# Attention scores of two heads as four products on the two 64-row halves of the matmul array

## The chip, the cores and the metric

The kernel runs on one core of a Trainium2 chip. A core has engines that run side by side, each with its own queue in fixed order: TensorE (PE, matmuls; its weight loads are shown apart as PEld), VectorE (DVE), ScalarE (ACT), GpSimd (POOL), and SyncE (SP), whose queue here issues all DMA transfers. Engines wait for each other by semaphores. The metric is the device time of one execution in microseconds (us); lower is better.

## The reference

A trunk of two layers over 1024 tokens of width 1024, with 16 heads of 64. Each layer adds a gated mixer to the residual stream.

```python
def reference(x, ...):
    for i in range(2):
        h = rms_norm(x, norm_g[i])
        o, gate = fox_mixer(h, ...) if i == 0 else dsw_mixer(h, cos, sin, ...)
        x = x + (o * silu(gate)) @ w_out[i]

def fox_mixer(h, w_in, b_f, q_g, k_g):        # layer 1: causal attention with forgetting
    q, k, v, gate, f = split(h @ w_in)        # q, k normed per head
    c = cumsum(log_sigmoid(f + b_f))          # per token and head
    s = q @ k.T * 64 ** -0.5 + c[q] - c[k]    # masked to keys <= query
    return softmax(s) @ v, gate

def dsw_mixer(h, cos, sin, w_in, q_g, k_g):   # layer 2: three groups of dilated windows
    for window, r in ((128, 1), (512, 4), (2048, 16)):
        # q, k normed and partly rotated; tokens r apart form a sequence of its own;
        # each query sees its own block of 128 keys and the block before, at most window // r back
        o_g, lse_g = banded_attention(q[g], k[g], v[g])
    return sum(softmax over g of lse_g * o_g), gate
```

All arithmetic is float32 in the reference. The kernel gets near that with split numbers: a value is written as a high and a low part, and products of parts are added.

## The kernel before

**Projections.** The input rows stand turned in SBUF as `xh` and `xl` (high and low part, tokens along the free axis). A projection of one tile of 128 tokens (`project`, L313) is 24 matmuls of 384 columns: eight blocks of the width, in each `xh` by the high and the low part of the weights and `xl` by the high part. After each six matmuls `flow.tick()` counts one slot, and what was filed for that slot with `flow.at` is written into PE's queue there: PE's order is the order of the program. So one projection tile is four slots. The other engines' orders are set by a scheduler at build time.

**The fox layer** goes over eight pairs of heads (`hp`), in each over eight tiles of 128 tokens (`t`). A projection tile gives q, k and v of two heads, k first. **The dilated layer** does the same for 24 pairs of heads and groups (`ci`); group 0 looks one block back, group 1 in every second tile, group 2 not at all.

**Heads.** For two tiles together, `heads_pair` norms and rotates q and k in `u` and writes `hl`, 16-bit: for each tile the high and low parts of k and q of both heads, `[hi(64), lo(64)]` for each head (L420 on ACT, L421 on POOL), and behind them, copied by DVE (L422), the parts of q swapped, `[lo, hi]`. One transposing DMA (L424) turns the twelve blocks into `qk_t`. In the fox layer POOL then copies the blocks of k into `kf` (L426), which holds the keys of one pair of heads side by side; the pool has two such buffers.

**Scores.** With 128 rows, `[hi, lo]` of q against `[hi, lo]` of k gives hi·hi + lo·lo, and the swapped q gives lo·hi + hi·lo: two matmuls for each head. In the fox layer `score(e, c)` does this for head `e` and a piece `c` of up to 512 keys (L619), adds the causal mask to the last block by a third matmul of an identity with `tri_b` (L622), and DVE adds the forgetting sums and takes the minimum (L624). It stands in slots of its own, one for each head and piece. In the dilated layer `score(i)` does tile `i` of the two for both heads, block by block (L798, DVE L801, ACT L802), tile 0 in one slot and tile 1 in the next.

**Behind the scores.** `p_transpose` takes exponentials (ACT, L467), writes them as high and low parts into `ph` (cast on ACT L470, difference on POOL L473; in the dilated layer L808 and L809) and turns `ph` into `ptt` by a transposing DMA (L474, L810). Some slots later `values` multiplies `ptt` by v: three matmuls of 64 or 65 columns for each block (`pv`, L481 to L483). For the fox tiles 0 to 3 both heads share one `ph` and one transposing DMA, from tile 4 on each head has its own. Tags `ph`, `p`, `ptt` and `kf` have 2, 4, 3 and 2 buffers in the first layer; the scores' PSUM pool `ps_s` has 3. The tag `kf` also serves the row of gains `gbc` of the second norm, which is loaded when the last fox projection has been issued and is read until the output projections end (L350).

Of the kernel before, what the change touches and what calls it, by code (L numbers as in the profile page):

```python
# [22 lines left out]
P = 128  # L23
# [59 lines left out]
def trunk(ctx, tc, ins, out, cfg):  # L83
# [52 lines left out]
    ident_b = const.tile([P, P], BF16, name="ident_b")  # L136
    nc.vector.tensor_copy(ident_b, ident)
    tri_b = const.tile([P, P], BF16, name="tri_b")
    nc.vector.tensor_copy(tri_b, tri)
# [45 lines left out]
    def rotary_tables():  # L185
# [5 lines left out]
        rt = lay([P, 5, 24, half], F32, name="rt", tag="kf")  # L191
# [161 lines left out]
    def load_gbc(layer):  # L353
        gbc = lay([P, D], F32, name="gbc", tag="kf")
# [41 lines left out]
    def heads_pair(gi, t, hd, kf):  # L396
# [24 lines left out]
        nc.gpsimd.tensor_sub(hl[:, :, :4, 1], u, hl[:, :, :4, 0])  # L421
        nc.vector.tensor_copy(hl[:, :, 4:], hl[:, :, 2:4, ::-1])  # L422
        qk_t = lay([P, 12, P], F16, name="qk_t", tag="qk_t")
        nc.sync.dma_start_transpose(qk_t, hl.rearrange("p i a b d -> p (i a b d)"))  # L424
        if kf is not None:
            nc.gpsimd.tensor_copy(  # L426
                kf[:, :, t * P : (t + 2) * P].rearrange("p e (i s) -> p i e s", i=2),
                qk_t.rearrange("p (i a) s -> p i a s", i=2)[:, :, :2],
            )
        return qk_t[:, :6], qk_t[:, 6:]  # L430
# [101 lines left out]
    def x_ready(t):  # L532
        if t + 2 < NT:
            load_xt(t + 2)
            split_xt(t + 2)
        if t + 1 < NT:
            row_factor(t + 1)
        if t == 1:
            load_gbc(0)
        if t == 3:  # L540
            gain_tables()
# [17 lines left out]
    def forget_sums():  # L559
        one = sb.tile([NH, 512], F32, name="one", tag="n2k", bufs=cfg["nb"])  # L560
        nc.vector.memset(one, 1.0)
        c = lay([NH, S], F32, name="fc", tag="kf")
# [32 lines left out]
    def fox_tile(hp, t, gs, qt, kf, vt, e0):  # L595
# [9 lines left out]
        def score(e, c):  # L605
            a, b = pieces[c]
            if c == 0:
                accs[e] = BIG
                st["acc"] = sm.tile([P, 2], F32, name="acc", tag="acc", bufs=8)
            if t < 2:  # L610
                if e == 0:
                    st["p"] = lay([P, 2, nk], F32, name="p", tag="p")
                p = st["p"][:, e]
            else:
                p = lay([P, b - a], F32, name="p", tag="p")
# [382 lines left out]
```

## Time and profile before

| | |
|---|---|
| median of 3 runs | 1849.05 us (1845.42 to 1851.41) |
| the profiled execution | 1848.65 us, its span 1846.9 us |
| PE busy | 1773.2 us, 13784 matmuls |
| DVE, ACT, POOL busy | 1101.9, 997.4, 976.0 us |
| DMA | 289.27 MB, 631429 packets, 510000 of them under 512 B |
| granted TensorE clock | 0.998 |

Spans on PE are pipelined: a matmul's length holds its way through the array, and the next starts long before it ends. So costs on PE are read from the distance between starts. Idle time of an engine counts only where PE waits in the end. In a row of the groups, behind the bar stand the busy time, the mean length in ns and the idle time before; `128*128` is the size of the stationary operand, the size behind it that of the moving one.

### The profile page before, as it was taken

The page shows a single profiled execution, that of the slowest core. Times are in us where ns is not written, and L with a number is a line of the kernel's source. Part 1 is how long each engine was busy: PE and PEld are TensorE (multiplying, and loading weights), DVE is VectorE, ACT ScalarE, POOL GpSimd, SP SyncE. Part 2 cuts the span into 40 slices and gives each one's busy share as a digit, 9 for nine tenths or more (in the row PEclk, how much of TensorE's full clock was granted, in tenths as well). Part 3 has the DMA queues.
Part 4 walks back from the last instruction along what each step waited for, and adds up shares of the span by engine and source line. Part 5 has one row for each costly group of instructions (what it writes and reads, how often), then busy time and mean ns, then how long its engine had stood idle before and what let it go on. Part 6 is the DMA issues. An engine that isn't in the chain of part 4 may idle for free.

```text
span 1846.9 us, 39170 instructions
## 1 busy us (share of the span) xinstructions
PE 1773.2 (96%) x13784; PEld 1648.0 (89%) x13784; DVE 1101.9 (60%) x3762; ACT 997.4 (54%) x2648; POOL 976.0 (53%) x1195
## 2 busy tenths in 40 slices
PE   6999999999988999999999999999999999999999
PEld 5997777877877889999999999999999999999899
DVE  7546655666657263356656666666676665766641
ACT  6535665666655254445655565555555555555520
POOL 4215665665654121255656655666576765766620
PEclk9999999999999999999999999999999999999999
DMA  8445988979999463346676686676776776667762
GB/s 268 124 125 127 187 176 171 190 172 181 191 174 226 135 224 126 102 110 151 130 141 132 142 183 146 141 156 148 141 147 153 165 151 139 151 148 166 167 167 92
DMA packets 631429, 289.27 MB, mean 157 GB/s; under 512 B 510000, under 2 KB 594992, under 8 KB 631232
## 3 DMA queue, kind: packets, MB, share of 16 engines
q1 hardware_dynamic: 631232, 286.77, 68.8%
q8 instruction: 108, 1.77, 0.4%
q14 instruction: 89, 0.73, 0.1%
HBM read 124.87 MB, written 37.03 MB: 88 GB/s over the span
## 4 chain that ended last, share of the span: by engine, by line
PE 52%; DMA 9%; DVE 4%; issue 3%; ACT 2%; POOL 2%; SPq 1%; POOLq 0%; DVEq 0%; ACTq 0%
PE pj L313 46%; PE s L798 3%; DMA raw<-in_w_dsw 2%; DMA ptt<-ph 2%; DMA qk_t<-hl 2%; DMA x_d<-xo 2%; POOL w L291 1%; PE ob L481 1%; PE ob L483 1%; PE ob L482 1%; PE pt L322 1%; DVE w L291 1%; DVE hl L422 0%; POOL hl L421 0%; DMA raw<-in_w_do 0%
## 5 line engine op out<-in xcount | busy, mean ns | idle before, releaser
L313 PE MATMUL pj<-w,xh 128*128 128x384 f32 (+2 forms) x5632 | 1472.2, 344 | 26.3 <-ACT w L289 11.7
L313 PEld LDWEIGHTS pj<-w,xh 128*128 128x128 f32 x5632 | 987.5, 191 | 49.4 <-ACT w L289 12.8
L313 PE MATMUL pj<-w,xl 128*128 128x384 f32 (+2 forms) x2816 | 940.3, 334 | 0.4 <-DVE xl L326 0.2
L313 PEld LDWEIGHTS pj<-w,xl 128*128 128x128 f32 x2816 | 535.5, 190 | 1.9 <-DVE xl L326 1.9
L291 POOL TENSOR_TENSOR w<-raw,w 128x384 fp32r<-128x384 f32 (+2 forms) x264 | 268.8, 1042 | 310.1 <-ACT w L289 303.2
L473 POOL TENSOR_TENSOR ph<-p,ph 128x512 f16<-128x512 f32 (+3 forms) x176 | 172.5, 994 | 127.3 <-ACT ph L470 105.0
L421 POOL TENSOR_TENSOR hl<-u,hl 128x512 f16<-128x512 f32 x128 | 150.2, 1173 | 143.9 <-ACT hl L420 143.8
L289 ACT CAST w<-raw 128x384 fp32r<-128x384 f32 (+2 forms) x352 | 160.8, 503 | 114.8 <-PE pj L313 39.9
L809 POOL TENSOR_TENSOR ph<-p,ph 128x768 f16<-128x768 f32 (+2 forms) x96 | 155.4, 1619 | 40.5 <-ACT ph L808 37.0
L481 PEld LDWEIGHTS <-ptt 128*128 128x128 f16 x1136 | 102.6, 98 | 67.7 <-DMA ptt<-ph 36.8
L802 ACT ACTIVATE p<-p,og 128x128 f32<-128x128 f32 (+1 forms) x256 | 100.9, 441 | 114.4 <-DVE og L801 112.6
L376 ACT ACTIVATE sq<-pj 128x256 f32<-128x256 f32 x256 | 96.9, 379 | 76.2 <-DVE u L371 75.0
L258 DVE TENSOR_REDUCE vm<-raw 128x1 f32<-128x256 f32 x128 | 53.6, 419 | 141.3 <-DMA raw<-in_w_dsw 112.8
L470 ACT CAST ph<-p 128x512 f16<-128x512 f32 (+3 forms) x176 | 88.7, 537 | 90.6 <-DMA ptt<-ph 89.6
L467 ACT ACTIVATE p<-p,acc 128x512 f32<-128x512 f32 (+2 forms) x192 | 110.9, 610 | 35.9 <-DVE acc L624 35.8
L420 ACT CAST hl<-u 128x512 f16<-128x512 f32 x128 | 79.5, 621 | 90.7 <-DVE u L418 73.7
L371 DVE TENSOR_TENSOR u<-pj,gr 128x256 f32<-128x256 f32 x256 | 106.8, 417 | 34.5 <-PE pj L313 33.9
L406 POOL TENSOR_TENSOR ra<-u,cs 128x128 f32<-128x128 f32 x96 | 44.5, 463 | 147.2 <-DVE u L371 145.2
L382 DVE SCALAR_TENSOR_TENSOR vt<-pj,vs,vt 128x128 f16<-128x128 f32 x192 | 67.2, 350 | 76.0 <-ACT vt L381 73.8
L482 PEld LDWEIGHTS <-ptt 128*128 128x128 f16 x1136 | 105.9, 97 | 1.7 <-issue 1.7
L483 PEld LDWEIGHTS <-ptt 128*128 128x128 f16 x1136 | 106.1, 97 | 0.0
L389 DVE TENSOR_REDUCE pj<-sq 128x8 f32<-128x512 f32 x128 | 88.3, 690 | 26.2 <-ACT sq L376 25.1
(170 smaller groups left out, 2424.4 us busy)
## 6 DMA issues: line engine op xcount, KB each, us to landing
raw<-in_w_dsw SPq DMA_DIRECT2D x96, 384.0 KB, 3.9
raw<-in_w_fox SPq DMA_DIRECT2D x32, 384.0 KB, 3.6
og_d<-og SPq DMA_DIRECT2D x64, 132.0 KB, 2.8
cmb<-og_d SPq DMA_DIRECT2D x64, 132.0 KB, 3.3
bc<-c_d SPq DMA_DIRECT2D x32, 256.0 KB, 5.2
gs_d<-ge SPq DMA_DIRECT2D x32, 192.0 KB, 2.5
xt<-in_xt SPq DMA_DIRECT2D x16, 256.0 KB, 4.0
xrow<-in_x SPq DMA_DIRECT2D x16, 256.0 KB, 4.0
```

The source lines that it names most:

```text
L289: nc.scalar.copy(w[:, 0, :n], raw[:, k % 2, :n])
L291: eng.tensor_sub(w[:, 1, :n], raw[:, k % 2, :n], w[:, 0, :n].bitcast(F32))
L313: nc.tensor.matmul(ps[:, :n], a[:, k, cols], w.slabs[k][:, j, :n], start=(k == 0 and i == 0), stop=(k == KT - 1 and i == 2))
L371: nc.vector.tensor_mul(u[:, t % 2].rearrange("p (a b) d -> p a b d", a=2), ps[:, : 4 * HD].rearrange("p (a b d) -> p a b d", a=2, b=2), gr ...
L421: nc.gpsimd.tensor_sub(hl[:, :, :4, 1], u, hl[:, :, :4, 0])
L467: nc.scalar.activation(p, p, AF.Exp, bias=acc, scale=-1.0)
L473: (nc.gpsimd if pool_l else nc.vector).tensor_sub(ph[:, e, 1, cols], p, ph[:, e, 0, cols])
L481: nc.tensor.matmul(o[:, e, :], hi, vt[:, j, e, HD:], start=(b == 0), stop=False, skip_group_check=True)
L482: nc.tensor.matmul(o[:, e, :HD], hi, vt[:, j, e, :HD], start=False, stop=False, skip_group_check=True)
L483: nc.tensor.matmul(o[:, e, :], lo, vt[:, j, e, HD:], start=False, stop=(b == n - 1), skip_group_check=True)
L802: nc.scalar.activation(p[:, e], p[:, e], AF.Exp, bias=acc[:, e : e + 1], scale=-1.0)
L809: nc.gpsimd.tensor_sub(ph[:, 1], st["p"], ph[:, 0])
```

## The change

`hl` now holds, for each tile, the high parts of k of both heads (128 wide), the low parts of both, and the same of q: four blocks instead of six. The swapped parts and L422 go. The transposing DMA turns eight blocks for two tiles instead of twelve, and puts head 0 on partitions 0 to 63 and head 1 on 64 to 127. `kf` and its copy (L426) go: keys are read from the `qk_t` of their two tiles, of which seven are kept in the first layer instead of three.

`scores` writes four products for each run of one or two key blocks (hi·hi, hi·lo, lo·hi, lo·lo), each as two matmuls of 64 rows in turn, one for each head, into two PSUM banks. So a run of keys takes eight matmuls, where two heads took four of 128 rows for any number of keys up to 512. The mask comes as two products of 64 rows for each head (`half_i`, `half_m`), which `mask_halves` makes on POOL and DVE in the first gate projection.

One call of `score` now does both heads. In the fox layer it takes a piece in one visit, the second piece two slots later (`pc=2`), and the values of both heads stand in one slot, `LS + LP + 4`, or `+ 3` for tiles 0 to 3, counted from `e0` (before `LS + LP + 2` and `+ 4` for the heads of tiles 4 to 7, and `+ 2` and `+ 3` for tiles 0 to 3). In the dilated layer both tiles of a pair are scored in one visit, at the slot where tile 1 stood. `ptt` has four buffers in the first layer instead of three. `gbc` and the rotary scratch `rt` move from the tag `kf` to `ph`, and `cmb` gets a tag of its own.

```diff
-        hl = sb.tile([P, 2, 6, 2, HD], F16, name="hl", tag="hl", bufs=cfg["hb"])
+        hl = sb.tile([P, 2, 2, 2, P], F16, name="hl", tag="hl", bufs=cfg["hb"])
         nc.vector.tensor_mul(u, u, y.unsqueeze(3).broadcast_to([P, 2, 4, HD]))
-        nc.scalar.copy(hl[:, :, :4, 0], u)
-        nc.gpsimd.tensor_sub(hl[:, :, :4, 1], u, hl[:, :, :4, 0])
-        nc.vector.tensor_copy(hl[:, :, 4:], hl[:, :, 2:4, ::-1])
-        qk_t = lay([P, 12, P], F16, name="qk_t", tag="qk_t")
+        uv = u.rearrange("p i (a e) d -> p i a (e d)", a=2)
+        nc.scalar.copy(hl[:, :, :, 0], uv)
+        nc.gpsimd.tensor_sub(hl[:, :, :, 1], uv, hl[:, :, :, 0])
+        qk_t = lay([P, 8, P], F16, name="qk_t", tag="qk_t")
         nc.sync.dma_start_transpose(qk_t, hl.rearrange("p i a b d -> p (i a b d)"))
-        if kf is not None:
-            nc.gpsimd.tensor_copy(
-                kf[:, :, t * P : (t + 2) * P].rearrange("p e (i s) -> p i e s", i=2),
-                qk_t.rearrange("p (i a) s -> p i a s", i=2)[:, :, :2],
-            )
...
+    def scores(ss, qk, i, keys, last):
+        prods = ((2, 0), (2, 1), (3, 0), (3, 1))
+        at = 0
+        for kk, j, cnt in keys:
+            for n, (qb, kb) in enumerate(prods):
+                for e in range(2):
+                    r = slice(HD * e, HD * e + HD)
+                    nc.tensor.matmul(
+                        ss[e][:, at * P : (at + cnt) * P].rearrange("p (c s) -> p c s", c=cnt),
+                        qk[r, i, qb],
+                        kk[r, j : j + cnt, kb],
+                        start=(n == 0),
+                        stop=(last and n == len(prods) - 1),
+                        skip_group_check=True,
+                    )
+            at += cnt
...
     def load_gbc(layer):
-        gbc = lay([P, D], F32, name="gbc", tag="kf")
+        gbc = lay([P, D], F32, name="gbc", tag="ph")
...
-            for i, blk in enumerate((2 + e, 4 + e)):
-                nc.tensor.matmul(s[:, : b - a], qt[:, blk], kf[:, e, a:b], ...)
+            ss = [ps_s.tile([P, 512], F32, name="s", tag="s") for e in range(2)]
+            runs = key_runs(range(a // P, b // P))
+            scores(ss, kts[t // 2], t % 2, [(kts[j // 2], j % 2, n) for j, n in runs], not last)
...
-        sl = e0 + LS
+        for c in range(len(pieces)):
+            urgent(lambda c=c: score(c), "ps", e0 + LS + cfg["pc"] * c)
         for e in range(2):
-            for c in range(len(pieces)):
-                urgent(lambda e=e, c=c: score(e, c), "ps", sl)
-                sl += 1
-            if not both:
-                urgent(lambda e=e: values(e), "pv", sl + LP)
-        if both:
-            for e in range(2):
-                urgent(lambda e=e: values(e), "pv", sl + LP + e)
+            urgent(lambda e=e: values(e), "pv", e0 + LS + LP + cfg["pe"][both][e])
...
-        for i in range(2):
-            urgent(lambda i=i: score(i), "ps", flow.now + LSD + i)
-        urgent(values, "pv", flow.now + LSD + LPD + 1)
+        urgent(score, "ps", flow.now + LSD)
+        urgent(values, "pv", flow.now + LSD + LPD)
...
-    lsd=((15, 12), (13, 11), (11, 9))    l1=dict(ga=7, kf=2, ptt=3, ph=2, p=4, qk_t=3)
+    lsd=((16, 12), (14, 11), (12, 9))    l1=dict(ga=7, ptt=4, ph=2, p=4, qk_t=7)    pc=2, pe=((4, 4), (3, 3))
```

**PE in the dilated layer, group 0 of one pair of heads.** Names with numbers are buffers; `s2` is a PSUM bank of scores, `pj` that of a projection. Before, the end of the scores of tile 0 of a pair of tiles and the start of those of tile 1:

```order
L798 LDWEIGHTS qk_t_14634
L798 MATMUL s2_14910<-qk_t_14634 128x128
L313 MATMUL pj_14868<-w_14725,xh_114 128x384 x2
L313 MATMUL pj_14868<-w_14725,xl_115 128x384
L313 MATMUL pj_14868<-w_14728,xh_114 128x384 x2
L313 MATMUL pj_14868<-w_14728,xl_115 128x384
L798 LDWEIGHTS qk_t_14634
L798 MATMUL s2_14929<-qk_t_14634 128x128
```

Now, the same border between tile 0 and tile 1 (`scores` is L461, the projection L328):

```order
L461 LDWEIGHTS qk_t_13220
L461 MATMUL s2_13487<-qk_t_13220 128x128
L461 LDWEIGHTS qk_t_13220
L461 MATMUL s2_13488<-qk_t_13220 128x128
L461 LDWEIGHTS qk_t_13220
L461 MATMUL s2_13487<-qk_t_13220 128x256
L461 LDWEIGHTS qk_t_13220
L461 MATMUL s2_13488<-qk_t_13220 128x256
```

The two heads alternate matmul by matmul between two banks, and no projection stands between the two tiles. Over the whole program PE leaves the projections 584 times before and 386 times now (stretches of other matmuls, counted in PE's queue); 192 of the 386 hold scores.

**POOL in the fox layer, first pair of heads,** tiles 4 and 5 (`hl` is L421, then L437; `ph` L473, then L512). Before:

```order
L473 TENSOR_TENSOR ph_1895<-p_1871,ph_1895 128x512
L473 TENSOR_TENSOR ph_1895<-p_1889,ph_1895 128x128
L473 TENSOR_TENSOR ph_1960<-p_1922,ph_1960 128x512
L473 TENSOR_TENSOR ph_1960<-p_1954,ph_1960 128x128
L426 COPY kf_1340<-qk_t_1796 128x2x2x128
L473 TENSOR_TENSOR ph_2019<-p_1976,ph_2019 128x512
```

Now:

```order
L512 TENSOR_TENSOR ph_1983<-p_1940,ph_1983 128x512
L512 TENSOR_TENSOR ph_1983<-p_1979,ph_1983 128x128
L512 TENSOR_TENSOR ph_1992<-p_1943,ph_1992 128x512
L512 TENSOR_TENSOR ph_1992<-p_1981,ph_1992 128x128
L512 TENSOR_TENSOR ph_2122<-p_2063,ph_2122 128x512
L512 TENSOR_TENSOR ph_2122<-p_2118,ph_2122 128x256
```

The copy of keys, which waits for a transposing DMA, is gone from between the differences.

**SP, the second pair of heads,** tiles 5 and 6. Before:

```order
L474 DMA_TRANSPOSE ptt_2924<-ph_2923 128x12x128
L474 DMA_TRANSPOSE ptt_2988<-ph_2987 128x12x128
L424 DMA_TRANSPOSE qk_t_2905<-hl_2900 128x12x128
L474 DMA_TRANSPOSE ptt_3028<-ph_3027 128x14x128
L664 DMA y_d_83<-y_3109 128x128
```

Now:

```order
L513 DMA_TRANSPOSE ptt_3146<-ph_3145 128x12x128
L439 DMA_TRANSPOSE qk_t_3110<-hl_3106 128x8x128
L513 DMA_TRANSPOSE ptt_3155<-ph_3154 128x12x128
L708 DMA y_d_83<-y_3339 128x128
L634 DMA bc_3512<-c_d_85 128x512
```

The transfer of q and k has eight blocks instead of twelve, and stands ahead of the second head's `ptt` instead of behind it.

More of the change, by code (lines that the diff above doesn't have):

```diff
@@ L539, in x_ready @@
             load_gbc(0)
+        if t == 2:
+            mask_halves()
         if t == 3:
@@ L626, in score @@
             pl = (cfg["pl"] & 1, cfg["pl"] >> 1 & 1)
-            if c < len(pieces) - 1 or both and e == 0:
-                return
             if both:
@@ L721, in trunk @@
                 with tc.high_priority(cfg["ph_"]):
-                    qts = heads_pair(0, t - 1, hd, kf)
-                for i, qt in enumerate(qts):
-                    fox_tile(hp, t - 1 + i, gsl[:, i], qt, kf, vt, flow.now - 4 + 4 * i)
+                    kts.append(heads_pair(0, t - 1, hd))
+                for i in range(2):
+                    fox_tile(hp, t - 1 + i, gsl[:, i], kts, vt, flow.now - 4 + 4 * i)
             if hp == NHP - 1:
```

123 lines of the change are left out of this document (71 added, 52 removed).

## The prediction

> **What bounds the kernel now.** I read the span on the page first, then the stages, the groups, the waits of the fox stage, and last the timeline of PE around single scores.
>
> ```profile
> span 1846.9 us, 39170 instructions
> ```
>
> ```profile
> core 0: us, PE busy (x) PEld busy (x) DVE busy (x) ACT busy (x) POOL busy (x), PEclk, DMA share, GB/s
> 0.00:40.00 40.00, 24.67 (x96) 20.57 (x96) 30.75 (x75) 23.88 (x63) 21.17 (x28) 1.00 0.82 262
> ...
> 138.00:545.00 407.00, 375.52 (x3383) 317.19 (x3383) 251.65 (x917) 250.60 (x619) 245.24 (x257) 0.99 0.87 175
> 700.00:1070.00 370.00, 368.98 (x2860) 356.12 (x2859) 207.35 (x661) 204.94 (x529) 187.33 (x226) 1.00 0.59 128
> 1070.00:1770.00 700.00, 693.17 (x5293) 658.02 (x5293) 458.37 (x1700) 388.42 (x1125) 448.95 (x609) 1.00 0.71 155
> ```
>
> PE bounds it. In the dilated layer (700 to 1770) PE idles 8 of 1070 us, so there only less work on PE, or fewer breaks in it, can bring anything. In the fox layer (138 to 545) PE idles 31.5 of 407 us, and the DMA engines are 0.87 busy, the highest share of any long stage. What PE waits for there:
>
> ```profile
> PE o L481 <- DMA ptt<-ph: 28.3, 23, 3.1
> PE s L619 <- POOL kf L426: 2.2, 2, 1.5
> ...
> ACT ph L470 <- DMA ptt<-ph: 84.3, 46, 4.0
> ...
> POOL kf L426 <- DMA qk_t<-hl: 29.0, 22, 4.2
> ...
> DVE p L624 <- POOL ph L473: 21.5, 22, 2.5
> ```
>
> 28.3 us go on `ptt`, the turned weights for the values. Their chain is DVE, ACT, POOL, SP, transposing DMA, and it is itself held up: ACT's cast waits 84.3 us until a `ph` buffer has been turned, and POOL stands 29.0 us in front of the copy into `kf`, with the differences that feed `ptt` queued behind it.
>
> **The price of a break.** Four, then eight matmuls of 128 columns amid projections:
>
> ```profile
> 1207.35 0.34 PE L313 MATMUL pj<-w,xl 128*128 128x384 f32 x1
> 1207.53 0.40 PE L798 MATMUL s<-qk_t 128*128 128x128 f16 x4
> 1207.74 0.61 PE L313 MATMUL pj<-w,xh 128*128 128x384 f32 x2
> 1208.19 0.34 PE L313 MATMUL pj<-w,xl 128*128 128x384 f32 x1
> ...
> 1208.72 0.34 PE L313 MATMUL pj<-w,xl 128*128 128x384 f32 x1
> 1208.90 0.62 PE L798 MATMUL s<-qk_t 128*128 128x128 f16 x8
> 1209.33 0.61 PE L313 MATMUL pj<-w,xh 128*128 128x384 f32 x2
> 1209.78 0.34 PE L313 MATMUL pj<-w,xl 128*128 128x384 f32 x1
> ```
>
> The columns are start, length, engine and group. From 1208.19 to 1208.72 three projection matmuls take 0.53. One score matmul is 0.22 long (221 ns below), so eight in 0.62 start 0.40/7 = 57 ns apart. The stretch with eight takes 1.06 from `xl` to `xl`; less 0.53 and 8 x 0.057 there remain 0.07. With four it is 0.84 - 0.53 - 0.23 = 0.08. So each visit away from the projections costs about 0.07 beyond its own matmuls.
>
> **The terms.** The groups that the change touches (behind the bar: busy time, mean ns, idle time before):
>
> ```profile
> L798 PE MATMUL s<-qk_t 128*128 128x128 f16 x1120 | 95.9, 221 | 5.1 <-DMA qk_t<-hl 5.1
> L619 PE MATMUL s<-kf,qk_t 128*128 128x512 f16 (+3 forms) x384 | 95.5, 330 | 3.1 <-POOL kf L426 2.2 <-DMA qk_t<-hl 0.8
> L422 DVE COPY hl<-hl 128x512 f16<-128x512 f16 x128 | 50.1, 391 | 57.3 <-POOL hl L421 55.9
> L426 POOL COPY kf<-qk_t 128x512 f16<-128x512 f16 x32 | 19.6, 611 | 32.9 <-DMA qk_t<-hl 32.8
> ```
>
> *Fewer breaks.* PE leaves the projections 386 times instead of 584: 198 x 0.07 = **-14**.
>
> *The scores themselves.* In units of 128 columns, before: fox 8 pairs x 36 blocks x 2 heads x 2 products = 1152, masks 128, dilated 1120, in all 2400 x 57 ns = 137 us. Now 2304 + 256 + 2240 = 4800 units on half the rows. If the two heads' halves run at once, that is 2400 units of time again, 137 us; if not, 137 us more. No row of before shows halves, so these are the ends: 0 and +137. What speaks for 0 beyond the arithmetic is only that consecutive matmuls use other rows and other PSUM banks. A bound for the issue comes from the values, which also load weights for every matmul:
>
> ```profile
> 1203.72 0.20 PE L481 MATMUL ob<-vt,ptt 128*128 128x65 f16 x1
> ...
> 1204.25 0.20 PE L483 MATMUL ob<-vt,ptt 128*128 128x65 f16 x1
> ```
>
> These are the first and the last of 18: 0.53/17 = 31 ns for a load and a matmul. Two of them take 62 against the 57 of a pair of 128 columns: 5 ns on 864 pairs (128 of fox blocks, 128 of masks, 608 dilated), none on the 768 pairs of 256 columns: **+4**. The Trainium skill's TensorE: Matmul & The Clock Gate (What overlaps and what doesn't) says that a weight load runs beside matmuls in flight only when their row groups differ; by it each half would stand still for its next load. The rows just quoted speak against it, since those loads and matmuls all use the same 128 rows and still pass every 31 ns.
>
> *The wait for `ptt` in the fox layer.* POOL loses the copy and the standing before it, 19.6 + 29.0 us of 407. The transposing DMAs of a pair of heads turn 144 blocks of `ph` (4 x 36) and 48 of q and k, now 32: 176 instead of 192, 8% less on the fullest resource. DVE loses L422 (391 ns for each two tiles) from the chain of `qk_t`. Against it: both heads now start together, so the second head's exponentials queue behind the first's on ACT, and tiles 4 to 7 take all four `p` buffers in the order head 0, head 1, head 0, head 1, so that DVE's next minimum waits for the second head's difference (the 21.5 us above grow, and DVE's queue with it). The values stand two slots later for head 0, in the same slot for head 1. The ends are -28 (all gone) and +14 (half as much again); I take half of it, **-14**, because two of the three links that wait (POOL, DMA) get shorter. L619's waits, 2.2 and 0.8, go with `kf`: **-2**.
>
> *The wait for `qk_t` in the dilated layer*, 5.1 us in L798's row: the first score of a pair moves one slot later and its chain loses L422 and a third of its blocks: **-4**, between -5 and 0. POOL, DVE and SP are not waited for by PE in that stage otherwise, so the later start of tile 0's exponentials (one slot, some 1.2 us) costs nothing as long as `ptt` stays ahead, as it is now.
>
> *The end of the fox layer.* `gbc` now takes one of the two `ph` buffers when the last projection is out, and keeps it. The transposes of tiles 4 to 7 of the last pair of heads come after that, eight of them, on one buffer. In that stretch (545 to 605):
>
> ```profile
> L474 SPq DMA_TRANSPOSE ptt<-ph x11: 1234/1882/4210, 545.5 to 594.1; - x11
> ...
> DMA to landing us min/median/max: 2.8/4.1/6.3
> L470 ACT CAST ph<-p x20: 294/605/619, 545.4 to 591.1; 128x512 f16<-128x512 f32 x12, 128x384 f16<-128x384 f32 x4, 128x128 f16<-128x128 f32 x2, 128x256 f16<-128x256 f32 x2
> L473 POOL TENSOR_TENSOR ph<-p,ph x21: 430/1162/1289, 544.4 to 592.6; 128x512 f16<-128x512 f32 x13, 128x384 f16<-128x384 f32 x4, 128x128 f16<-128x128 f32 x2, 128x256 f16<-128x256 f32 x2
> ```
>
> On one buffer each must pass cast (0.6), differences (1.2 to 2.3) and landing (2.8 to 4.1) before the next cast: 4.6 to 7.0, eight times 37 to 56 us. Now the 11 of the row take from 545.5 to 594.1 and 4.1 to land, 52.7; eight elevenths of that are 38. So 0 to 18 us are added, and PE reaches these values in order, with the turned rows of the output projection behind them. SP's loads of `xr` and `yt` queue behind the late transposes too. I take **+8**.
>
> *Free:* `mask_halves`, eight small operations on POOL in the first gate projection, where POOL is about half idle (21.17 of the first 40 us); without that cover some 5 us, at 0.6 each as for L426. `ptt`'s fourth buffer and seven `qk_t` only loosen. Three PSUM score buffers against two for each visit: the next visit is two slots away, two minima (0.6 each) earlier; nothing, unless DVE stands.
>
> Sum: -14 + 4 - 14 - 2 - 4 + 8 = -22. Against the span 1846.9 that is 1825; the profiled execution has 1.75 outside its span, so **1827 us**. The median of the runs, 1849.05, is 0.4 above this execution. Less than 0.3% (5.5 us) can't be told from no change.
>
> **Rivals.**
>
> *PE must run empty at each change of form* (the other side). Scores use half the rows, all else uses 128, so 192 visits change the form twice. A 128-column score is 221 ns long and the next starts after 57, so 164 are still under way: up to 384 x 0.164 = 63 us, 1827 + 63 = **1890**. It turns the gain from 57 ns a change on. The Trainium skill's TensorEngine Tiling (Array Packing), Key Properties, states such a drain. Before has one visit in another form, `128*16`:
>
> ```profile
> 88.44 0.34 PE L313 MATMUL pj<-w,xl 128*128 128x384 f32 x1
> 88.62 1.03 PE L566 MATMUL pz<-ident,zt 128*16 128x128 f32 x8
> 89.41 0.60 PE L313 MATMUL pj<-w,xh 128*128 128x384 f32 x2
> 89.85 0.34 PE L313 MATMUL pj<-w,xl 128*128 128x384 f32 x1
> ```
>
> From `xl` to `xl` 1.41; less 0.53 it leaves 0.88 for eight, 0.11 each, which is what their starts are apart (1.03 less a matmul of about 0.27, over 7). No room for 0.3 of emptying; but this narrows columns, not rows, and it is one visit. Chance 0.12, of it 0.04 for a part that ends within 0.3% of before.
>
> *The halves don't run at once*: 1827 + 137 - 4 = **1960**. For it: nothing of before shows that they do. Chance 0.07.
>
> *Each half stands for its load*: at most 31 ns (the values' distance) on 1632 pairs, 50 us, 1827 + 50 - 4 = **1873**. Chance 0.04, for the reason above.
>
> *The fox chain is not relieved*: starting both heads together eats what POOL and the DMA save, and the end of the layer costs more: 1827 + 14 + 12 = **1853**, no change. For it: ACT is on the chain with 84.3 us of waiting for `ph`, of which there are still two. Chance 0.19, a third of it slower than 1855.
>
> *The fox chain comes free*, as the DMA share falls and POOL never stands: 1827 - 14 - 8 = **1805**. Chance 0.16.
>
> **How the numbers follow.** The forecast, 1815 to 1843, has 0.42; with the freed chain 0.58 are faster by over 0.3%, and 0.02 of the unrelieved chain's near side: 0.60. Within 0.3%: 0.11 of the unrelieved chain and 0.04 of the drain, 0.15. Slower: 0.08 drain, 0.07 no overlap, 0.04 loads, 0.06 chain, 0.25. The range from 1800 to 1862 leaves out 0.03 below and about 0.17 above.
>
> **What would show it.** Two score matmuls of the two heads starting close together and a pair of 256 columns every 110 to 120 ns show the overlap; 0.07 of remainder per visit shows that no drain is paid, 0.2 to 0.4 that it is. PE's wait for `ptt` in the fox layer should be near 14, POOL's wait for `qk_t` gone, the DMA share a little lower. Eight transposes some 5 to 7 us apart at the fox layer's end, with ACT's cast waiting for each, show the single buffer. The prediction is wrong if scores take much over 140 us of PE's starts, or if PE's fox waits stay at 28.

## The result, and the profile after

The change makes the kernel slower: 1900.18 us median of 4 runs (1896.96 to 1906.78) against 1847.24 us (1842.65 to 1851.41) for the kernel before. The ratio is 1.0292, 95% interval 1.0254 to 1.0330. The prediction, 1827 us and faster, has the wrong sign, and the result lies outside its range of 1800 to 1862.

Two windows of the profile after, the prediction's fox stage and the stretch behind it, and then the second one in the profile before:

```profile
core 0: us, PE busy (x) PEld busy (x) DVE busy (x) ACT busy (x) POOL busy (x), PEclk, DMA share, GB/s
138.00:545.00 407.00, 385.44 (x4135) 341.05 (x4136) 235.16 (x863) 243.25 (x604) 221.43 (x223) 0.98 0.79 160
545.00:700.00 155.00, 130.05 (x1139) 119.75 (x1138) 67.92 (x203) 60.86 (x141) 42.67 (x44) 0.94 0.65 167
```

```profile
545.00:700.00 155.00, 140.49 (x1056) 127.12 (x1055) 85.36 (x233) 72.46 (x171) 45.61 (x49) 1.00 0.71 193
```

In the fox window PE is busier than before (385.44 against 375.52) although it gets less far. DVE, ACT and POOL are all less busy there, and the DMA share fell from 0.87 to 0.79, so none of them has become the limit by its load; whether PE waits for one of them is told by the waits. The scores' group, and then PE's waits over the whole program (us in total, times, longest):

```profile
L461 PE MATMUL s<-qk_t 64*128 64x128 f16 (+1 forms) x3008 | 163.7, 245 | 21.6 <-DVE acc L667 21.5
```

```profile
PE s L461 <- DVE acc L667: 21.5, 12, 3.3
PE o L520 <- DMA ptt<-ph: 14.8, 12, 5.9
...
PE ob L520 <- DMA ptt<-ph: 5.5, 5, 2.7
```

The wait of the fox layer's values for `ptt` was halved (14.8, 28.3 before), but PE now waits 21.5 us for DVE to empty a score bank, for which the profile before has no row. The three rows make 41.8 us, where before the rows for `ptt`, `qk_t` and `kf` made 36.4 (28.3 + 5.1 + 0.8 + 2.2). So waits alone can't explain 53 us. Where the time is lost is seen better from the lengths of the stages. The table counts PE's projection matmuls and takes the time from the first of a stage to the first of the next, so that the same work is compared; the last row is what is left between the first projection matmul of the program and the last. It is read from one trace each, and has two of the experiments beside the two kernels:

| us | before | after | whole products | gains in a buffer of their own |
|---|---|---|---|---|
| fox layer | 435.1 | 449.1 | 423.7 | 453.5 |
| end of the fox layer (its output projection) | 132.8 | 150.0 | 149.6 | 139.1 |
| dilated layer | 961.9 | 978.2 | 948.9 | 977.1 |
| all the rest | 304.7 | 306.9 | 309.2 | 306.2 |

So 14 us were lost in the fox layer, 17 at its end and 16 in the dilated layer (the two traces are 48 us apart, the medians 53).

A part of the first two is the clock. At the end of the fox layer the column PEclk fell from 1.00 to 0.94. The trace's clock record has it as stretches of 3.4 or 6.8 us at half clock; before has two of them (6.8 us, both in the fox layer), the kernel after nine (five in the fox layer and four at its end, 17 us each, none in the dilated layer). Each of the nine begins 2 to 4 us after PE began a wait of about 2 us or more, but not every such wait is followed by one. In such a stretch a projection follows the other in 0.32 us instead of 0.175:

```profile
634.09 0.52 PE L328 MATMUL pj<-w,xl 128*128 128x384 f32 x1
634.41 0.84 PE L328 MATMUL pj<-w,xh 128*128 128x384 f32 x2
635.05 0.52 PE L328 MATMUL pj<-w,xl 128*128 128x384 f32 x1
```

So up to 45% of a stretch is lost. As an estimate that is at most 5 us more than before in the fox layer (17 against 6.8 us of such stretches) and 7 at its end, where PE idles for 2 of the 17 anyway.

In the dilated layer PE's waits for other engines are nearly as before (8.3 us from 700 to 1740, 6.6 before), so there it is likely that the visits themselves have become dearer. This is PE's timeline around one visit of the dilated layer in the kernel after, 24 products in 12 pairs:

```profile
1015.72 0.34 PE L328 MATMUL pj<-w,xl 128*128 128x384 f32 x1
1015.99 1.06 PE L461 MATMUL s<-qk_t 64*128 64x128 f16 x24
1016.97 0.62 PE L328 MATMUL pj<-w,xh 128*128 128x384 f32 x2
1017.44 0.34 PE L328 MATMUL pj<-w,xl 128*128 128x384 f32 x1
```

From `xl` to the scores it takes 0.27 us, where projections follow each other every 0.17 to 0.18. Singly, the records show the two heads' matmuls starting 3 to 4 ns apart and the pairs every 56 ns (128 columns) or 109 ns (256 columns). So the overlap of the two halves is full, and no weight load stands in its way (two loads of 94 ns belong to each pair). From `xl` to `xl` it is 1.72 us; less 0.53 for the three projections and 8 x 0.056 + 4 x 0.109 = 0.88 for the pairs, 0.31 remain, where the kernel before had 0.07. The prediction had written that 0.2 to 0.4 here would show the emptying of PE.

### The profile page after: what moved, and what is told of

Its sections match the earlier page's. It is cut to its first block, busy times and chain, and to the rows that moved or that the text cites. A ratio compares the mean times of both kernels' runs of the same rounds, so it can differ in the third digit from the quotient of the medians.

```text
span 1895.2 us, 42233 instructions
## 1 busy us (share of the span) xinstructions
PE 1817.3 (96%) x15416; PEld 1694.9 (89%) x15416; DVE 1044.1 (55%) x3637; ACT 984.4 (52%) x2648; POOL 957.4 (51%) x1171
## 4 chain that ended last, share of the span: by engine, by line
PE 55%; DMA 17%; POOL 8%; issue 7%; ACT 6%; DVE 5%; SPq 2%; POOLq 0%; ACTq 0%; DVEq 0%
PE pj L328 48%; DMA ptt<-ph 8%; DMA raw<-in_w_fox 3%; PE s L461 3%; POOL ph L512 3%; POOL w L306 3%; DMA raw<-in_w_dsw 2%; ACT ph L509 2%; ACT p L506 2%; POOL hl L437 1%; DMA x_d<-xo 1%; DVE p L667 1%; PE ob L520 1%; PE ob L522 1%; PE ob L521 1%
## 5 line engine op out<-in xcount | busy, mean ns | idle before, releaser
L328 PE MATMUL pj<-w,xh 128*128 128x384 f32 (+2 forms) x5632 | 1458.3, 342 | 23.3 <-ACT w L304 10.5
L328 PEld LDWEIGHTS pj<-w,xh 128*128 128x128 f32 x5632 | 997.4, 191 | 60.5 <-issue 14.0
L328 PE MATMUL pj<-w,xl 128*128 128x384 f32 (+2 forms) x2816 | 941.6, 334 | 0.1
L328 PEld LDWEIGHTS pj<-w,xl 128*128 128x128 f32 x2816 | 537.5, 191 | 0.4 <-DVE xl L341 0.4
L512 POOL TENSOR_TENSOR ph<-p,ph 128x512 f16<-128x512 f32 (+3 forms) x176 | 170.7, 991 | 189.6 <-ACT ph L509 167.6
L437 POOL TENSOR_TENSOR hl<-u,hl 128x512 f16<-128x512 f32 x128 | 150.6, 1177 | 99.3 <-ACT hl L436 97.9
L461 PE MATMUL s<-qk_t 64*128 64x128 f16 (+1 forms) x3008 | 163.7, 245 | 21.6 <-DVE acc L667 21.5
L461 PEld LDWEIGHTS <-qk_t 64*128 64x128 f16 x3008 | 108.1, 94 | 71.8 <-issue 61.1
L520 PEld LDWEIGHTS <-ptt 128*128 128x128 f16 x1136 | 104.5, 99 | 49.0 <-DMA ptt<-ph 25.8
L506 ACT ACTIVATE p<-p,acc 128x512 f32<-128x512 f32 (+2 forms) x192 | 105.5, 606 | 39.6 <-DVE acc L667 38.9
L839 ACT ACTIVATE p<-p,og 128x128 f32<-128x128 f32 (+1 forms) x256 | 102.3, 441 | 36.8 <-DVE og L838 36.4
L521 PEld LDWEIGHTS <-ptt 128*128 128x128 f16 x1136 | 107.0, 98 | 1.3 <-issue 1.3
```

What stands on the lines that cost most here:

```text
L328: nc.tensor.matmul(ps[:, :n], a[:, k, cols], w.slabs[k][:, j, :n], start=(k == 0 and i == 0), stop=(k == KT - 1 and i == 2))
L437: nc.gpsimd.tensor_sub(hl[:, :, :, 1], uv, hl[:, :, :, 0])
L461: nc.tensor.matmul(ss[e][:, at * P : (at + cnt) * P].rearrange("p (c s) -> p c s", c=cnt), qk[r, i, qb], kk[r, j : j + cnt, kb], start=(n ...
L506: nc.scalar.activation(p, p, AF.Exp, bias=acc, scale=-1.0)
L512: (nc.gpsimd if pool_l else nc.vector).tensor_sub(ph[:, e, 1, cols], p, ph[:, e, 0, cols])
L520: nc.tensor.matmul(o[:, e, :], hi, vt[:, j, e, HD:], start=(b == 0), stop=False, skip_group_check=True)
```

## Experiments

**1. Whole products.** Theory 1: PE runs empty when the form changes. Theory 2: the loss lies in the buffers and in DVE. In this kernel the order, the visits, the buffers and the passes of columns of the change stay; each pair of 64-row products becomes one product of 128 rows. It leaves out half of the score products and mixes the heads, so its time is no time for the task.

```diff
-                for e in range(2):
-                    r = slice(HD * e, HD * e + HD)
-                    nc.tensor.matmul(ss[e][...], qk[r, i, qb], kk[r, j : j + cnt, kb], start=(n == 0), ...)
+                e = n % 2
+                nc.tensor.matmul(ss[e][...], qk[:, i, qb], kk[:, j : j + cnt, kb], start=(n < 2), ...)
```

> The changed kernel, in which every pair of 64-row score products (one per head, on the two halves of the array) is one product of all 128 rows; so is each pair of mask products. The number of passes of columns, the visits, the buffers, the transfers and the work of DVE, ACT and POOL stay. It leaves out half of the score products and mixes the heads in the others, so its time is no time for the task. Theory 1 (PE runs empty when the rows of a product change from 128 to 64 and back): the remainder per score visit falls from 0.30 us back to 0.07, which over 192 visits is 45 us, so about 1855 us. Theory 2 (the loss comes from DVE's late minimum, the third PSUM buffer and the end of the fox layer, the form costs nothing): only the issue of 864 products goes, under 5 us, so 1895 to 1900.

Measured: 1843.3 us, ratio to before 0.9970 (0.9954 to 0.9986), 57 us less than the changed kernel and 12 below theory 1's 1855. A visit with the same passes as the one above, and then this kernel's largest waits of PE:

```profile
1003.80 0.34 PE L328 MATMUL pj<-w,xl 128*128 128x384 f32 x1
1003.97 1.06 PE L460 MATMUL s<-qk_t 128*128 128x128 f16 x12
1004.79 0.60 PE L328 MATMUL pj<-w,xh 128*128 128x384 f32 x2
1005.23 0.34 PE L328 MATMUL pj<-w,xl 128*128 128x384 f32 x1
```

```profile
PE s L460 <- DVE acc L664: 25.6, 18, 3.4
PE o L519 <- DMA ptt<-ph: 17.5, 8, 5.8
```

The twelve whole products take the same 1.06 as the twelve pairs, but the stretch from `xl` to `xl` is 1.43 instead of 1.72. The missing 0.29 is 0.10 on the way in (0.17 against 0.27), 0.16 on the way out (0.82 from the first score to the next projection, against 0.98) and 0.03 at the second projection. Of the 0.31 that remained, 0.02 are left, not the 0.07 that theory 1 took. Times 192 visits that is 56 us, and 57 were measured. The fox layer's waits for DVE and for `ptt` didn't shrink (they grew by 4 and 3 us; the dilated values' wait for `ptt` fell from 5.5 to 1.2), so it isn't they that moved. The dilated layer is the cleaner test: no stretch at half clock in either trace, and 96 visits of 0.29, so 28 us, against 29.3 in the table. In the fox layer the 25.4 us are a balance: 28 for the visits, up to 8 for the 17 us at half clock, of which this kernel has none there, and the other way 9 for its longer waits (30.5 against 21.4 in the window of the prediction). So the agreement of 56 with 57 is in part luck. Theory 1 holds; theory 2 is out as the main cause.

**2. Two visits again.** If each visit pays, more visits must pay more. Here the products of tile 0 get a visit of their own.

```diff
+        urgent(lambda: products(0), "ps", flow.now + LSD - 1)
         urgent(score, "ps", flow.now + LSD)
```

> The changed kernel, in which the score products of a dilated piece are issued in two visits again, as in the kernel before: the same products, 96 visits more, so 192 changes of form more. Theory 1 (each visit with a change of form costs 0.30 us beside its products, 0.235 of it the change): 96 x 0.30 = 29 us longer, about 1929. Theory 2 (a visit costs the 0.07 of any visit): 7 us longer, about 1907. If the score banks' wait for DVE is relieved by taking the two tiles apart, some 5 us less in both.

Measured: 1923.32 us, ratio 1.0408 (1.0382 to 1.0435), 23 us above the changed kernel: 96 more visits at 0.24 each. The dilated layer alone grew by 21.8 (978.2 to 1000.0). This is on theory 1's side (29, or 24 with the relief of the banks; 7 without the price), and PE's wait for the score banks gave back 3.9, near the 5 expected:

```profile
PE s L461 <- DVE acc L667: 17.6, 10, 3.6
```

**3. The gains in a buffer of their own.** The end of the fox layer lost its 17 us in the run with whole products too (149.6), so it has another cause. To make room, `qk_t` has six buffers here instead of seven and `ra` and `rb` one each.

```diff
-        gbc = lay([P, D], F32, name="gbc", tag="ph")
+        gbc = lay([P, D], F32, name="gbc", tag="gbc")
-    l1=dict(ga=7, ptt=4, ph=2, p=4, qk_t=7)    ra, rb: bufs=2
+    l1=dict(ga=7, ptt=4, ph=2, p=4, qk_t=6, gbc=1)    ra, rb: bufs=1
```

> The changed kernel with a buffer of its own for gbc (it shared the two buffers of ph); to make room, qk_t has 6 buffers instead of 7 and ra and rb one instead of two. Theory A (the 17 us that the last part of the fox layer and its output projection lost come from the eight transposes that then have one ph buffer): 10 to 17 us faster, 1883 to 1890. Theory B (they come from the form of the products and from DVE's late minima there): no more than 4 us faster. Against both: one ra buffer may hold POOL up, which would cost a few us.

Measured: 1886.21 us, ratio 1.0205 (1.0181 to 1.0229), 14 us less than the changed kernel; the end of the layer takes 139.1 instead of 150.0 (by these traces the fox layer ahead of it is 4 us longer). The transposing DMAs and ACT's casts there, first in the changed kernel and then here:

```profile
L513 SPq DMA_TRANSPOSE ptt<-ph x9: 1315/1567/1754, 569.9 to 628.2; - x9
...
  ACT ph L509: 14.0, 7
  PEld L520: 6.7, 2
  PE o L520: 6.2, 2
```

```profile
L513 SPq DMA_TRANSPOSE ptt<-ph x10: 1273/1802/4787, 562.0 to 614.4; - x10
```

The indented rows say who waited for these DMAs. With one `ph` buffer the transposes are 58.3/8 = 7.3 us apart, ACT's next cast waits for seven of them, 14.0 us in all, and PE's values for two, 6.2 us. With two they are 52.4/9 = 5.8 apart, and ACT and PE have no such rows; PE's 8.7 us of waits for DVE at the score banks there are gone too. Theory A holds. The size, 11 by the stage and 14 by the medians, lies in the upper part of the 0 to 18 that the prediction gave, of which it took 8. Of the 17 us some 6 stay (139.1 against 132.8). This run has 16 us at half clock there, like the changed kernel, and before none; that is worth up to 7, so it can be the rest, though no run takes it away by itself.

**4. Four score banks.** The pool of PSUM has no spare bank, so the fourth is taken from the output of the values.

```diff
-    ps_s = pool("ps_s", 3, PSUM)
-    ps_o = pool("ps_o", 2, PSUM)
+    ps_s = pool("ps_s", 4, PSUM)
+    ps_o = pool("ps_o", 1, PSUM)
```

> The changed kernel with four score banks in PSUM instead of three and one bank for the values' output instead of two. Theory A (PE's 21.5 us of waits for DVE's minimum at the score banks are what the merged visit lost, and a fourth bank takes them away): 12 to 20 us faster, 1880 to 1888. Theory B (DVE's minimum is late in any case and the wait moves to the values, or the single output bank makes the values wait): within 5 us, or slower.

Measured: 1910.28 us, ratio 1.0338 (1.0293 to 1.0382), 10 us slower than the changed kernel. PE's wait for DVE at the score banks has no row any more, but the wait for `ptt` has doubled:

```profile
PE o L520 <- DMA ptt<-ph: 29.8, 23, 5.8
PE pt L337 <- DVE xl L341: 12.3, 10, 3.6
```

The fox layer is no shorter (452.0). The likely reading is that the scores there are ahead of a chain that can't turn the weights faster, so that the wait only changes its place; but the run changes two pools at once, and doesn't show it alone. The dilated layer lost 15 us; the turned rows `pt` (L335) can use the output bank too, and their wait grew from 3.4 to 12.3, nearly all of it in the dilated layer (0.4 to 9.1). It also has 10 us at half clock there, after waits of 3.3 and 3.6 us, where the changed kernel has none. How much of the loss is the single output bank isn't told apart.

**5. The price of a form by itself.** The kernel before, with one more matmul in the middle of each of the 96 values visits of the dilated layer, into columns that nobody reads: in the form of the neighbours, with 64 rows, and with 32 columns.

```diff
                     pv(o[:, i], e, [...], vt)
+                    if i == 0 and e == 1:
+                        nc.tensor.matmul(ob[:, 448:512], pt[:, 0, 0], vt[:, t0, 0, :64], ...)       # neighbours' form
+                        nc.tensor.matmul(ob[:, 448:512], pt[:64, 0, 0], vt[:64, t0, 0, :64], ...)   # or: 64 rows
+                        nc.tensor.matmul(ob[:32, 448:512], pt[:, 0, 0, :32], vt[:, t0, 0, :64], ...)  # or: 32 columns
```

> The kernel before, with one more matmul in the middle of each dilated piece's values visit (96 of them): 128 rows, 128 columns of weights, 64 columns streamed into a part of the output bank that nobody reads. It keeps the form of its neighbours and is the scale for the two kernels beside it. Every theory: 64 columns are 27 ns and the weights take about as long again, so 96 x 0.03 to 0.06 = 3 to 6 us longer than before, 1850 to 1854.

> The same extra matmul with 64 rows instead of 128 (both operands cut to the first 64 partitions). Theory 1 (going to 64 rows and back costs 0.29 us, as between the changed kernel and the one with whole products): 96 x 0.29 = 28 us longer than the kernel with the 128-row extra, about 1880. Theory 2 (that price belongs to two heads' halves working at once, or to the score visits, not to the number of rows as such): no more than 5 us from the 128-row extra.

> The same extra matmul with 128 rows but only 32 columns of weights. Theory 1a (PE runs empty at any change of form, the narrow one too): 28 us longer than the kernel with the 128-row, 128-column extra, about 1880. Theory 1b (only a change of the rows empties it; the mask visit with 128*16 in the profile showed no such gap): no more than 3 us from that kernel, 1848 to 1854.

Measured: 1854.34 us (1.0041, 1.0024 to 1.0058), 1869.40 (1.0115, 1.0095 to 1.0135) and 1869.56 (1.0111, 1.0088 to 1.0134). The extra matmul L822 between its neighbours, in their form and then with 64 rows:

```profile
920.48 0.20 PE L483 MATMUL ob<-vt,ptt 128*128 128x65 f16 x1
920.51 0.19 PE L822 MATMUL ob<-vt,ptt 128*128 128x64 f16 x1
920.54 0.19 PE L481 MATMUL ob<-vt,ptt 128*128 128x65 f16 x1
```

```profile
923.81 0.20 PE L483 MATMUL ob<-vt,ptt 128*128 128x65 f16 x1
923.94 0.20 PE L822 MATMUL ob<-vt,ptt 64*128 64x64 f16 x1
924.07 0.20 PE L481 MATMUL ob<-vt,ptt 128*128 128x65 f16 x1
```

In the neighbours' form the starts are 0.03 us apart; with 64 rows they are 0.13 apart on both sides. Each change costs 0.10, with no second head, no minimum and no buffer in play. The run with 32 columns has the same distances. So theory 1a holds in kind: rows and columns cost the same. In size it doesn't: 28 us were expected from the 0.29 amid projections, and here a visit costs 0.20. All 96 visits show it alike, 0.26 from neighbour to neighbour against 0.06 in the neighbours' form, so the 64-row run should be 96 x 0.20 = 19 us above the other; it is 15 by the medians. The difference lies in the run in the neighbours' form: against before, the 64-row run is 22 us longer (1869.40 against 1847.51), and its 96 visits are 96 x (0.26 - 0.03) = 22, but the run in the neighbours' form is 7 longer where its visits explain 3. Why isn't known.

**6. Why the mask visit had shown no gap.** The prediction had leaned on eight `128*16` operations without a gap. They differ from the 32-column matmul in width, in type (f32) and in being transposes: L566 writes `nc.tensor.transpose`, and the profile prints both as MATMUL. The same place again, with 16 columns of f16, and with an f32 transpose of 16 and of 32 columns.

```diff
+                        nc.tensor.matmul(ob[:16, 448:512], pt[:, 0, 0, :16], vt[:, t0, 0, :64], ...)   # f16, 16 columns
+                        nc.tensor.transpose(ob[:16, 384:512], ident[:, :16], ident)   # f32 transpose, 16 columns; or 32
```

> The kernel before with the extra f16 matmul of the 32-column run, now with 16 columns of weights, the width of the mask visit in the profile of before. Theory A (PE runs empty for 32 columns but not for 16, because 16 columns run in the form of the whole array): no gap, as with 128 columns, 1850 to 1856, and the weights are loaded about 100 ns before the matmul. Theory B (16 columns of f16 empty it like 32, and the visit in the profile escaped for its f32 operands): 1866 to 1872, and the load starts within 10 ns of its matmul, some 125 ns after the start of the matmul ahead.

> In place of that extra matmul a transpose of 16 columns of the f32 identity, 128 columns streamed: the very form of the mask visit in the profile of before, now between f16 matmuls. An f32 transpose takes 0.11 us by that visit and its load as long, so 10 to 20 us longer than before without a gap, 1858 to 1867 (theory A for the width, theory B for the type, both without a gap). Theory C (that visit escaped because its neighbours were f32 too): 20 us more, 1878 to 1887, with the load held back.

> The same transpose with 32 columns of the identity. Theory A (32 columns are a form of their own, 16 are not): 15 to 20 us longer than the 16-column transpose, the load held back by 0.1 us. Theory B (f32 operands escape): the same time as the 16-column transpose within 3 us.

Measured: 1868.49 us (1.0117, 1.0098 to 1.0136), 1858.49 (1.0059, 1.0043 to 1.0074) and 1859.30 (1.0073, 1.0059 to 1.0086). First 16 columns of f16, then the f32 transpose, each with the load of its weights (PEld) in a fence behind it:

```profile
920.39 0.20 PE L483 MATMUL ob<-vt,ptt 128*128 128x65 f16 x1
920.51 0.20 PE L822 MATMUL ob<-vt,ptt 128*16 128x64 f16 x1
920.64 0.20 PE L481 MATMUL ob<-vt,ptt 128*128 128x65 f16 x1
```

```profile
920.51 0.09 PEld L822 LDWEIGHTS <-ptt 128*16 128x16 f16 x1
```

```profile
921.98 0.20 PE L483 MATMUL ob<-vt,ptt 128*128 128x65 f16 x1
922.02 0.27 PE L822 MATMUL ob<-ident 128*16 128x128 f32 x1
922.12 0.19 PE L481 MATMUL ob<-vt,ptt 128*128 128x65 f16 x1
```

```profile
921.98 0.10 PEld L822 LDWEIGHTS ob<-ident 128*16 128x16 f32 x1
```

The f16 matmul's load is held until 0.12 after the start of the matmul ahead. The transpose's load starts with the matmul ahead, and the next matmul follows 0.11 after it (108 ns in the records), the distance between the transposes of the mask visit. So it isn't the width, and the mask visit didn't escape because of its neighbours. What was left was type or transpose: f32 matmuls that are no transposes.

```diff
+                        nc.tensor.matmul(ob[:32, 448:512], ident[:, :32], ident[:, :64], ...)   # f32, 32 columns
+                        nc.tensor.matmul(ob[:, 448:512], ident[:64], ident[:64, :64], ...)      # or: f32, 64 rows
+                        nc.tensor.matmul(ob[:, 448:512], ones[:64], ones[:64, :64], ...)        # or: fp32r, 64 rows
```

> The kernel before with the extra instruction in the middle of each dilated values visit as an f32 matmul, not a transpose: 32 columns of the identity as weights, 64 columns streamed. Theory B (f32 operands escape the emptying): its weights are loaded some 35 ns before it starts and 1 to 5 ns after the start of the matmul ahead, as in the f32 transposes; the time is 1850 to 1865 by how long an f32 matmul of 64 columns takes. Theory T (transposes escape, matmuls don't): the load is held until some 125 ns after the start of the matmul ahead, as with f16, and the same on the way out, 20 us more.

> The same f32 matmul with 64 rows and 128 columns of weights. Theory B: the load is not held back, as with 32 columns. Theory R (rows are split in any type, columns only in f16): the load is held some 125 ns after the start of the matmul ahead, 20 us more than a run in which it isn't.

> The same with 64 rows in fp32r, the type of the projections. Theory B: the load is not held back. Theory R: it is held some 125 ns.

Measured, in two runs each: 1873.23, 1878.91 and 1877.32 us; before was 1839.72 beside them (ratios 1.0177, 1.0208 and 1.0200). The first:

```profile
864.89 0.19 PE L483 MATMUL ob<-vt,ptt 128*128 128x65 f16 x1
865.01 0.30 PE L822 MATMUL ob<-ident 128*32 128x64 f32 x2
865.25 0.20 PE L481 MATMUL ob<-vt,ptt 128*128 128x65 f16 x1
```

It is held by 0.12 like f16, and so are both kinds with 64 rows. Theory T: a matmul pays in every type that was tried, and the transpose doesn't. Against before it costs 33.5 us, the transpose of 32 columns 12.8: the 20 us of that theory, though the two also differ in columns and in passes, so the held load is the firmer sign. The Trainium skill's TensorEngine Tiling (Array Packing), Gotcha 2: Feature Incompatibilities, says that the narrow columns of a tiled array and an f32 transpose exclude each other. By it the mask visit can only have run in the form of the whole array, and the traces agree, as far as they show two widths without a gap. The Trainium skill's TensorEngine Tiling (Array Packing), Key Properties, asks for a drain at each change of mode without a price; here it is 0.10 us a change between f16 matmuls of 64 columns.

**7. The rest of the change without the form.** The merged visits, keys read from `qk_t`, but the 128-row products of before with the swapped parts of q, and `ptt=3`, `qk_t=6`. Then the same with `gbc` in its own buffer (`qk_t=5`, `ra` and `rb` one each).

```diff
-            for n, (qb, kb) in enumerate(prods):
-                for e in range(2):
-                    ... qk[r, i, qb], kk[r, j : j + cnt, kb] ...
+            for e in range(2):
+                for n, qb in enumerate((2 + e, 4 + e)):
+                    ... qk[:, i, qb], kk[:, j : j + cnt, e] ...
```

> The changed kernel's order (both tiles' scores in one visit, no copy of the keys) with the products of the kernel before: 128 rows, the swapped parts of q made by DVE and transposed with the rest, one mask product per head; qk_t has 6 buffers and ptt 3, since the 12-block qk_t is larger. It computes what the reference asks for. Theory 1 (the form was the loss, the merged visits are a small gain): the stages up to the last part of the fox layer fall by 0.29 us x 192 against the changed kernel, the transfer of the swapped parts comes back and with it some of PE's waits for ptt, so 1840 to 1855; the tail of the fox layer keeps its 17 us. Theory 2 (the merged visits or the missing copy cost as much as the form): above 1865.

> The merged visits with 128-row products, as in the run with whole products that computes what is asked for, and gbc in a buffer of its own (qk_t has 5 buffers, ptt 3, ra and rb one each). Theory A (the two losses, the form and the single ph buffer at the end of the fox layer, are independent): 11 to 14 us less than that run's 1858, so 1844 to 1847, no different from the kernel before. Theory B (the end of the layer loses as much by the merged visits themselves, or five qk_t buffers hold the dilated layer up): 1855 or more.

Measured: 1858.16 us, ratio 1.0062 (1.0037 to 1.0086), and 1836.47 us, ratio 0.9942 (0.9926 to 0.9958). The first is 3 us above the 1840 to 1855 expected and slower than before: its fox and dilated layers are shorter (429.2 and 958.0), but it keeps the long end of the fox layer (151.1). The second gets that back (134.8, before 132.8), has a shorter fox layer (426.4 against 435.1) and a shorter dilated layer (955.8 against 961.9), and is 10 us faster than the kernel before, 0.6%. It gained 22 us over the first, where 11 to 14 were expected; of that 16 lie in the end of the layer, where the buffer was meant to act, and there the stretches at half clock also fell from 24 to 14 us, up to 5 of the 16. Its waits:

```profile
PE o L504 <- DMA ptt<-ph: 16.8, 12, 3.5
...
PE s L445 <- DVE acc L647: 11.7, 15, 1.6
```

## Why the prediction was wrong

*The step that failed* is in the rivals: *PE must run empty at each change of form*, which had the right mechanism and nearly the right price (63 us; 57 measured), got a chance of 0.12. The price came near by some luck: it took 0.164 for each change, where 0.10 were measured on the way in and 0.19 on the way out. It was put down by one row, the eight `128*16` operations without a gap, with the reservation that this "narrows columns, not rows, and it is one visit". That was the wrong reservation. Narrow columns pay the same as half the rows (experiment 5), and the row was no witness at all, because it holds transposes (experiment 6). The sum had nothing for this: 57 of the 75 us between -22 and the measured +53, or 56 by the visits.

*The end of the fox layer*: the mechanism was right, the size was not. +8 was taken, 14 measured by experiment 3 (11 by the stage), within the ends of 0 to 18. The transposes are 7.3 us apart, where 5 to 7 were expected. By the medians that is 6 us more than the sum had.

*Three PSUM score buffers: "nothing, unless DVE stands".* DVE stood. PE waits for `acc` 21.5 us, of which 12.8 lie in the window of the fox layer (8 waits of up to 2.3) and 8.7 at its end, where they go with the buffer of the gains (experiment 3). With two banks for each visit, a third leaves one of the next visit's two dependent on DVE's last minimum. But in experiment 4 these microseconds were not simply to be had: without them the wait for `ptt` rose instead.

*The wait for `ptt`*: -14 was taken for the fox window. It went from 28.3 to 8.6 there, so -19.7, better than forecast, but the wait for DVE above took 12.8 of it, and the dilated layer's values now wait 5.5 for `ptt`, where nothing was expected ("as long as `ptt` stays ahead"). 12.8 + 5.5 - 5.7 = 12.6 us worse than the sum. With 57 and 6 that makes 76 of the 75, a match that is luck in part: these waits are read from one trace each, the 57 are a balance in the fox layer (experiment 1), the sum's +4 for the issue of the halves came out at nothing (pairs of 128 columns stand 56 ns apart, not 62), and the stretches at half clock, at most 12 us more than before, had no term of their own.

*Right:* the scores themselves. The halves overlap fully, pairs of 256 columns stand 109 ns apart (110 to 120 forecast), so the rivals *The halves don't run at once* and *Each half stands for its load* are out. *Fewer breaks* and the wait for `qk_t`: with whole products the dilated layer is 13.0 us shorter than before, where 96 visits x 0.07 and 4 make 11. POOL's wait for `qk_t` is gone with the copy, and the DMA share fell. Without the price of the form the forecast would still have been too low: 1843.3 with whole products, against 1827.

## What to carry to other kernels

Packing two 64-row products side by side is free while they run, but each visit in another form costs PE about 0.2 us between f16 matmuls and 0.29 us amid projections. Here the passes of columns were as many after as before, so the form could only lose; elsewhere it must save more than that in each visit, or all of PE's work must have the same form. Before a row of a profile is used as a witness against a mechanism, look in the code whether it is the same operation: the profile calls a transpose and a matmul by the same name. And when a tile is moved to another buffer's tag, count who uses those buffers from then until it is released.

## What was not expected of the hardware

- A change of form is paid on both sides and at the same price for 64 rows and for 16 or 32 columns: 0.10 us each way between f16 matmuls. Amid projections the way in costs 0.10 and the way out 0.19, so 0.29 for a visit. In the records of the dilated visits the held load starts 0.071 to 0.072 before the end that the profile gives the matmul ahead, on the way in and on the way out; in experiments 5 and 6 it is the same (0.195 - 0.123). With whole products it starts 0.16 and 0.27 before that end. These ends are modelled, so the traces don't show whether PE is quite empty at that moment.
- f32 transposes of 16 or 32 columns don't pay it: they start 0.03 to 0.04 us after the f16 matmul ahead. Whether transposes of 64 rows or of f16 do wasn't tried.
- Two 64-row matmuls on the two halves start 3 to 4 ns apart and take no longer than one of 128 rows: 1.06 us for 12 pairs and for 12 whole products.
- In the changed kernel nine of the twelve waits of PE of about 2 us or more from 100 us on were followed by 3.4 or 6.8 us at half clock, with projections 0.32 us apart instead of 0.175. Before it was two of ten. What decides it isn't shown.
